# Dividing the softmax before its transposes, and a PSUM tile each for the gate and up products, in a two-layer diffusion trunk

## The chip, the cores and the metric

The kernel runs on one core of one Trainium2 chip. The metric is device time in microseconds (us), from the first to the last instruction of the program with what the runtime adds around it; a time given as "before" is the median of three runs. All data is float32 in the chip's main memory, about 480 MB of it read once.

## The reference, cut to what matters

Two layers run over 256 latent tokens and 256 context tokens of width 1024. Each layer projects the normalised tokens to three head groups (A: global attention of 6 heads, B: a 31-tap convolution with a normalisation behind it, C: windowed attention of 6 heads with a learned sink per head), multiplies their concatenation by `w_out`, adds it to the residual, and then applies a mixture of 32 experts, of which each token uses two. The last layer keeps only the latent tokens. What the change touches is the softmax and the first half of an expert:

```python
sc = jnp.einsum('bqhgd,bkhd->bhgqk', qblk, k_all).astype(jnp.float32) * ATTN_SCALE
p = jax.nn.softmax(sc, axis=-1).astype(v_all.dtype)
return jnp.einsum('bhgqk,bkhd->bqhgd', p, v_all)
...
def run(args):
    xb, e = args
    return (jax.nn.silu(xb @ w_gate[e]) * (xb @ w_up[e])) @ w_down[e]
```

## The kernel before, in words

**Layers and stages.** `layer(l)` is run for `l` = 0 and 1. In each: modulation and input projections; the attention stage; the output projection with `w_out` (line 952); the router; then 16 pairs of experts. Layer 0 handles four tiles of 128 tokens, layer 1 two.

**Attention.** `unit(g, j, i)` handles two heads (`h` = 0 and 1) of one block of queries. For `i` = 0 and 1 it is one latent block against 512 keys (`nb` = 1); for `i` = 2, in layer 0 alone, it is both context blocks against 256 keys each (`nb` = 2). Layer 0 has 18 units (12 with `nb` = 1, 6 with `nb` = 2), layer 1 has 12 (all `nb` = 1). TensorE makes the scores S (lines 819 to 822), VectorE takes their row maxima (825), ScalarE writes P = exp(S - max) and the row sums `lsum`, one head after the other (839), VectorE takes the reciprocals `rl` (848). TensorE transposes P by head (853), VectorE and ScalarE copy one head's PT each (854), TensorE multiplies by V into `po` (860). Two times `nb` more products by the identity spread `rl` along the free axis in the other half of `po` (866; each is two instructions). ScalarE copies that into `ars` (870), VectorE multiplies (871), and the result is split into a rounded high part (873, ScalarE) and a remainder (874, VectorE). The buffers of `ars` and `gpad`, the padded input of the convolution, lie in pools that close with the stage; line 1020 opens a pool for the weight tile `xs` after them, and its load (line 1021) is the first of a row of loads in SyncE's queue.

**What sets the order there.** SyncE's queue is in the order of the program. The other engines' order in the attention stage is chosen at build time by the framework's planner, from the order of the program and from its own estimate of when operands are ready. The convolution is 62 VectorE instructions on `gpad` and `ca` in a serial chain (`tap`, lines 641 and 643); those that are left when the units begin (`conv(len(taps))`, line 876) are spread among them. `conv_norm` follows with line 783 on the last tap, and its result is what the last two of eight parts of the output projection need.

**Expert pairs.** `pair` takes two experts, which use the two 64-column halves of the array. Weights come in tiles of 1 MB through a ring of eight, loaded ahead by SyncE; a slot is loaded again as soon as the products that read it are done. A pair uses 12 of them: four each for gate, up and down. The PSUM pool `P2` has two buffers of two banks each. Before the change one P2 tile `pgu` holds the gate product in its first bank and the up product in its second (line 1354), and another one, `py`, holds the down product (line 1408). ScalarE takes SiLU of the gate half (1358) when its 16 products are done; `burst(0)` then issues work of other pairs; the up products follow; VectorE multiplies both (1363); `split_y` (1275, 1276) empties `py`. In this loop the order on TensorE, VectorE and ScalarE is that of the program, and `burst(0)` to `burst(3)` mark the places where the gathers of the next quad and the scatter of the pair before are put. In layer 0, for pairs 1 to 13 of 0 to 15, `burst(0)` holds at most one VectorE instruction (`onehot`); in layer 1 it holds three scatter products of the pair before.

The framework adds the waits: an instruction that writes a tile waits for those that read or wrote that tile before, and a tile from a pool waits until the readers of the buffer's last tile are done.

Of the kernel before, what the change touches and what calls it, by code (L numbers as in the profile page):

```python
# [10 lines left out]
F32 = mybir.dt.float32  # L11
# [4 lines left out]
OP = mybir.AluOpType  # L16
# [20 lines left out]
def trunk(ctx: ExitStack, tc: tile.TileContext, t_in, rope, out, cfg):  # L37
# [426 lines left out]
    def layer(l):  # L464
# [343 lines left out]
        def unit(g, j, i):  # L808

            nb = 1 if i < 2 else 2
            S = P2("S")
            for b in range(nb):
                for h in range(2):
                    q, kv = qT[g](2 * j + h, 128 * (i + b)), (2 * j + h) // 3
                    masked = g == 1 and i < 2
                    o, ks = (S[:, h, :], slice(0, 512)) if i < 2 else (S[:, h, 256 * b:256 * b + 256], slice(256, 512))
                    pe.matmul(o, q, kH[g][:, kv, ks], start=True, stop=False)
                    pe.matmul(o, q, kL[g][:, kv, ks], start=False, stop=not masked)  # L820
                    if masked:
                        pe.matmul(S[:, h, 128 - 128 * i:256 - 128 * i], identb, masks[:, i], start=False, stop=True)
            n = 2 * nb
            mx = sm.tile([128, 4], F32, name="mx")[:, :n]
            ve.tensor_reduce(mx, S.rearrange("p h (b k) -> p (h b) k", b=nb), axis=AX.X, op=OP.max)
            nm = sm.tile([128, 4], F32, name="nm")[:, :n]
            ns = negsink[:, l, j, :, None].to_broadcast([128, 2, nb])
            if g == 1:
                ve.scalar_tensor_tensor(nm.rearrange("p (h b) -> p h b", b=nb), mx.rearrange("p (h b) -> p h b", b=nb),
                                        -SCALE, ns, op0=OP.mult, op1=OP.min)  # L830
            else:
                ve.tensor_scalar(nm, mx, -SCALE, None, op0=OP.mult)
            P = K4("P", (128, 2, 512))
            lsum = sm.tile([128, 4], F32, name="lsum")[:, :n]
            w_ = 512 // nb
            for h in range(2):
                for b in range(nb):
                    e = h * nb + b
                    sc.activation(P[:, h, w_ * b:w_ * b + w_], S[:, h, w_ * b:w_ * b + w_], AF.Exp,
                                  bias=nm[:, e:e + 1], scale=SCALE, accum_out=lsum[:, e:e + 1])  # L840
            if g == 1:
                es = sm.tile([128, 4], F32, name="es")[:, :n]
                ve.tensor_tensor(es.rearrange("p (h b) -> p h b", b=nb), nm.rearrange("p (h b) -> p h b", b=nb), ns,
                                 op=OP.subtract)
                sc.activation(es, es, AF.Exp)
                ve.tensor_tensor(lsum, lsum, es, op=OP.add)
            rl = sm.tile([128, 4], F32, name="rl")[:, :n]
            ve.reciprocal(rl, lsum)
            PT = K4("PT", (128, 2, 512))
            for h in range(2):  # L850
                pt = P1("pT")
                for kt in range(4):
                    pe.transpose(pt[:, 128 * kt:128 * kt + 128], P[:, h, 128 * kt:128 * kt + 128], ident)
                (sc.copy if h else ve.tensor_copy)(PT[:, h], pt)
            po = P1("po")
            for b in range(nb):
                for kt in range(4 // nb):
                    for h in range(2):
                        cv_ = 128 * g + 64 * ((2 * j + h) // 3)
                        pe.matmul(po[64 * h:64 * h + 64, 128 * b:128 * b + 128],  # L860
                                  V[:, kt if i < 2 else 2 + kt, cv_:cv_ + 64],
                                  PT[:, h, 128 * (b * 2 + kt):128 * (b * 2 + kt) + 128],
                                  start=kt == 0, stop=kt == 4 // nb - 1)
            for b in range(nb):
                for h in range(2):
                    pe.matmul(po[64 * h:64 * h + 64, 256 + 128 * b:384 + 128 * b],
                              rl[:, h * nb + b:h * nb + b + 1].to_broadcast([128, 64]), ident, start=True, stop=True)
            nq = 128 * nb
            rs = K2("ars", (128, nq), tag="a")
            sc.copy(rs, po[:, 256:256 + nq])  # L870
            ve.tensor_tensor(rs, po[:, 0:nq], rs, op=OP.mult)
            mh = qT[g](2 * j, 128 * i, nq)
            sc.copy(mh, rs)
            ve.tensor_tensor(qT[g](2 * j + 1, 128 * i, nq), rs, mh.bitcast(F32), op=OP.subtract)

        conv(len(taps))
        n = 0
# [466 lines left out]
        def pair(pr, xg, ws, burst, final, finish):  # L1344


            p = P2("pgu")
            for m in range(2):
                for a in range(2):
                    w_ = (load_rows_two([weights_of(pr, m, a, e) for e in range(2)], "we") if final else  # L1350
                          [weight(m, a, e, pr) for e in range(2)])
                    for k in range(4 * a, 4 * a + 4):
                        for e in range(2):
                            pe.matmul(p[64 * e:64 * e + 64, m, :], xg[:, k, 64 * e:64 * e + 64], w_[e](k % 4),  # L1354
                                      start=k == 0, stop=k == KC - 1)
                if m == 0:
                    sil = K2("sil", tag="w")
                    sc.activation(sil, p[:, 0], AF.Silu)  # L1358
                    if final:
                        sqrt_table(sil)  # L1360
                    burst(0)
            act = K2("act", tag="w")
            ve.scalar_tensor_tensor(act, p[:, 1], ws, sil, op0=OP.mult, op1=OP.mult)  # L1363
            burst(1)
            pt = P1("pat")
            for f in range(4):
                pe.transpose(pt[:, 128 * f:128 * f + 128], act.rearrange("s (a p k) -> s a k p", a=2, k=2)[:, f // 2, f % 2], ident)  # L1367
            actT = K2("actT", tag="w")
            sc.copy(actT, pt)  # L1369
            burst(2)  # L1370
            tiles = y_tiles()
            oht = K2("oht", (128, 512), F32R)

            def slots():
                pb = P1("pb")
                se = sm.tile([32, 2, 64], F32R, name="se")
                gp.tensor_copy(se, ident[:32, 2 * pr:2 * pr + 2, None].to_broadcast([32, 2, 64]))  # L1377
                pe.matmul(pb[:, :N], se.rearrange("p a b -> p (a b)"), posT[:, :N], start=True, stop=True)  # L1378
                ve.tensor_scalar(oht[:, :N], pb[:, :N], slotid, None, op0=OP.is_equal)

            def products(py, wd, fs):
                for f in fs:
                    for e in range(2):
                        pe.matmul(py[64 * e:64 * e + 64, :], actT[:, 128 * f + 64 * e:128 * f + 64 * e + 64],  # L1384
                                  wd[e](f), start=f == 0, stop=f == 3)

            slots()
            if final:
                for h in range(2):
                    py = P2("py")[:, 0]  # L1390
                    wd = load_rows_two([down_half(h, e, pr) for e in range(2)], "we")
                    products(py, wd, range(2))
                    if h == 0:
                        burst(3)
                    else:
                        finish(0, tiles, oht[:, :N], py)
                    products(py, wd, range(2, 4))
                    if h == 0 or not last:
                        split_y(py, h, 128, tiles)
                finish(1, tiles, oht[:, :N], py)  # L1400
                return []
            py = P2("py")
            for a in range(2):
                wd = [weight(2, a, e, pr) for e in range(2)]
                for f in range(2 * a, 2 * a + 2):
                    for h in range(2):
                        for e in range(2):
                            pe.matmul(py[64 * e:64 * e + 64, h], actT[:, 128 * f + 64 * e:128 * f + 64 * e + 64],  # L1408
                                      wd[e](f % 2)[:, 512 * h:512 * h + 512], start=f == 0, stop=f == 3)
                if a == 0:  # L1410
                    burst(3)
            for h in range(2):
                split_y(py[:, h], h, 128, tiles)
            return row_adders(tiles[0], tiles[1], oht[:, :N])
# [277 lines left out]
```

## Time and profile before

| what | value |
|---|---|
| median of 3 runs | 1475.16 us (1473.77 to 1477.0) |
| the profiled execution's own time | 1472.71 us |
| its span, first to last instruction | 1470.7 us |
| TensorE busy (matmul), share of the span | 1390.8 us, 95% |
| VectorE busy | 613.4 us, 42% |
| ScalarE busy | 395.7 us, 27% |
| mean granted TensorE clock | 0.986 |
| bytes read from main memory | 479.42 MB |

The profile is of one execution. A matmul's end is modelled and matmuls overlap, so TensorE's busy share says little about how full it is; the waits and the start times say more. PE stands for TensorE's matmuls, PEld for its weight loads, DVE for VectorE, ACT for ScalarE, POOL for GpSimd, SP for SyncE and its queue of loads. Layer 0's attention stage lies at about 142 to 240 us of the span, its expert pairs at about 300 to 800; layer 1's attention stage at about 895 to 950, its pairs at about 990 to the end.

### The profile page before, as it was taken

The numbers are of one execution on the slowest core, as the hardware profiler recorded it, in microseconds if no ns is written. First come the engines' busy times: TensorE is split into PE (matmuls) and PEld (weight loads), VectorE is DVE, ScalarE is ACT, GpSimd is POOL, SyncE is SP. The second block draws the span as 40 slices with busy tenths as digits, with TensorE's granted clock in tenths as the row PEclk, the third lists the DMA queues.
The fourth block names the chain that finished last, engine by engine and source line by source line (L and its number), as shares of the span: only waits on it lengthen the run. The fifth ranks groups of instructions, "written<-read, shape, count | busy, mean of one in ns | idle before, by whom it ended". The sixth has DMA issues, their size and how long they took to land. (4 is left out here: it accounts for less than half of the span.)

```text
span 1470.7 us, 20485 instructions
## 1 busy us (share of the span) xinstructions
PE 1390.8 (95%) x8068; PEld 771.3 (52%) x8068; DVE 613.4 (42%) x1380; ACT 395.7 (27%) x954; POOL 76.7 (5%) x132
## 2 busy tenths in 40 slices
PE   6999999999999999999998998889999999999987
PEld 5776677755445544444434776783433343333332
DVE  4379974443323423233325679853222222222223
ACT  4454675421111111101102565552111011111102
POOL 1202000100000000000001110010000000000000
PEclk9999999999999999999999999999999999999999
DMA  9757204397999999999999590186999999999996
GB/s 350 282 166 284 109 1 172 131 375 306 376 408 414 413 400 406 417 406 414 385 405 389 201 332 31 44 357 280 388 422 421 421 421 421 421 421 419 421 417 255
DMA packets 97412, 481.86 MB, mean 328 GB/s; under 512 B 14068, under 2 KB 22544, under 8 KB 52128
## 3 DMA queue, kind: packets, MB, share of 16 engines
q1 hardware_dynamic: 96576, 478.79, 81.1%
q8 instruction: 66, 1.08, 0.3%
q10 hardware_dynamic: 464, 1.11, 0.2%
q0 software_dynamic: 272, 0.59, 0.1%
q14 instruction: 34, 0.28, 0.0%
HBM read 479.42 MB, written 1.05 MB: 327 GB/s over the span
## 5 line engine op out<-in xcount | busy, mean ns | idle before, releaser
L1354 PE MATMUL pgu<-we,xg 128*64 128x512 f32 x1904 | 449.3, 598 | 30.7 <-DMA we<-in_w_gate_dram 13.6
L1354 PEld LDWEIGHTS pgu<-we,xg 128*64 128x64 f32 x1904 | 142.3, 137 | 324.1 <-issue 246.8
L1408 PE MATMUL py<-we,actT 128*64 128x512 f32 x888 | 202.9, 596 | 0.7 <-ACT actT L1369 0.7
L1363 DVE SCALAR_TENSOR_TENSOR act<-pgu,ws,sil 128x512 f32<-128x512 f32 x32 | 24.0, 751 | 285.1 <-PE pgu L1354 248.6
L1250 DVE SCALAR_TENSOR_TENSOR xT<-pc,mod,xT 128x256 f32<-128x256 f32 x256 | 104.8, 477 | 52.9 <-PE pc L1247 52.2
L1408 PEld LDWEIGHTS py<-we,actT 128*64 128x64 f32 x888 | 63.1, 137 | 117.5 <-issue 113.4
L1304 ACT COPY xg<-pg 128x256 f32<-128x256 f32 x112 | 36.3, 376 | 308.2 <-PE pg L1300 308.2
L1258 DVE TENSOR_TENSOR xo<-xo,pc 128x512 f32<-128x512 f32 x62 | 39.8, 684 | 112.0 <-PE pc L1257 112.0
L1299 PE MATMUL pg<-OH,hH 128*128 128x256 f32 x336 | 83.3, 286 | 0.0
L1300 PE MATMUL pg<-OH,hL 128*128 128x256 f32 x336 | 82.1, 283 | 0.0
L643 DVE SCALAR_TENSOR_TENSOR ca<-gpad,cw,ca 128x512 f32<-128x512 f32 (+1 forms) x120 | 74.2, 619 | 0.9
L1299 PEld LDWEIGHTS pg<-OH,hH 128*128 128x128 f32 x336 | 63.9, 190 | 7.2 <-issue 5.7
L1300 PEld LDWEIGHTS pg<-OH,hL 128*128 128x128 f32 x336 | 64.1, 191 | 0.9
L1358 ACT ACTIVATE sil<-pgu 128x512 f32<-128x512 f32 x32 | 19.1, 598 | 167.6 <-PE pgu L1354 167.6
L281 PE MATMUL pm<-wm,scT 128*32 128x256 f32 (+1 forms) x896 | 60.7, 359 | 3.0 <-DMA wm<-in_w_mod_dram 2.8
L1273 DVE TENSOR_TENSOR Yg<-py,g2r 128x512 f32<-128x512 f32 x31 | 21.3, 688 | 100.7 <-PE py L1408 96.4
L1276 DVE TENSOR_TENSOR YL<-py,YH 128x512 fp32r<-128x512 f32 x32 | 22.1, 690 | 92.7 <-ACT YH L1275 92.7
L1275 ACT CAST YH<-Yg 128x512 fp32r<-128x512 f32 x31 | 19.1, 617 | 141.2 <-DVE Yg L1273 141.2
L1275 ACT CAST YH<-py 128x512 fp32r<-128x512 f32 x32 | 18.7, 585 | 139.0 <-PE py L1408 113.8
L1377 POOL CAST se<-ident 32x128 fp32r<-32x128 f32 x32 | 9.1, 287 | 900.1 <-PE pb L1378 900.1
L1246 PE MATMUL pc<-oht,YH 128*128 128x512 f32 x128 | 53.4, 418 | 1.2 <-ACT YH L1275 1.2
L1247 PE MATMUL pc<-oht,YL 128*128 128x512 f32 x128 | 50.6, 395 | 0.2 <-DVE YL L1276 0.2
(429 smaller groups left out, 2106.0 us busy)
## 6 DMA issues: line engine op xcount, KB each, us to landing
we<-in_w_up_dram SPq DMA_DIRECT2D x112, 1024.0 KB, 9.7
we<-in_w_down_dram SPq DMA_DIRECT2D x111, 1024.0 KB, 12.4
we<-in_w_gate_dram SPq DMA_DIRECT2D x110, 1024.0 KB, 13.5
wm<-in_w_mod_dram SPq DMA_DIRECT2D x44, 1024.0 KB, 9.4
wp<-in_w_gate_dram SPq DMA_DIRECT2D x8, 1024.0 KB, 9.5
wp<-in_w_up_dram SPq DMA_DIRECT2D x8, 1024.0 KB, 9.7
we<-in_w_gate_dram SPq DMA_DIRECT2D x16, 512.0 KB, 12.1
we<-in_w_up_dram SPq DMA_DIRECT2D x16, 512.0 KB, 10.2
```

Source lines behind the costliest of these rows:

```text
L281: pe.matmul(p[0][32 * q:32 * q + 32], scT[:, kq, :], ws[128 * kq // nr][:, kq % (nr // 128), c:c + n], start=k == 0, stop=k == KC * nq // ...
L643: ve.scalar_tensor_tensor(a, g, wt, a, op0=OP.mult, op1=OP.add)
L1246: pe.matmul(pc, YH[:, 128 * o:128 * o + 128], oht, start=True, stop=False)
L1247: pe.matmul(pc, YL[:, 128 * o:128 * o + 128], oht, start=False, stop=True)
L1250: ve.scalar_tensor_tensor(xT[:, o, sl], pc[:, sl], mod[l][:, 5, o, s:s + 1], xT[:, o, sl], op0=OP.mult, op1=OP.add)
L1258: ve.tensor_tensor(xo[t][:, sl], xo[t][:, sl], pc, op=OP.add)
L1275: sc.copy(YH[:rows, sl], py)
L1299: pe.matmul(dst, hH[t][:, 128 * k:128 * k + 128], rhs, start=t == 0, stop=False)
L1300: pe.matmul(dst, hL[t][:, 128 * k:128 * k + 128], rhs, start=False, stop=t == NT - 1)
L1304: sc.copy(xg[e][:, k - 1:k + 1, :], v[:, :, e])
L1354: pe.matmul(p[64 * e:64 * e + 64, m, :], xg[:, k, 64 * e:64 * e + 64], w_[e](k % 4), start=k == 0, stop=k == KC - 1)
L1408: pe.matmul(py[64 * e:64 * e + 64, h], actT[:, 128 * f + 64 * e:128 * f + 64 * e + 64], wd[e](f % 2)[:, 512 * h:512 * h + 512], start=f == ...
```

## The change

In `unit`, P is multiplied by the reciprocals of its row sums in place, one head on VectorE and one on ScalarE, one instruction for each block, ahead of the transposes. The products that spread `rl`, the copy `ars` and the multiplication by it fall away; the high part is copied and the remainder is subtracted straight from `po` in PSUM. In `pair`, each of the gate and the up product gets a P2 tile of its own and uses its first bank.

```diff
             rl = sm.tile([128, 4], F32, name="rl")[:, :n]
             ve.reciprocal(rl, lsum)
+            for h in range(2):
+                for b in range(nb):
+                    e = h * nb + b
+                    p = P[:, h, w_ * b:w_ * b + w_]
+                    if h:
+                        sc.activation(p, p, AF.Identity, scale=rl[:, e:e + 1])
+                    else:
+                        ve.tensor_scalar(p, p, rl[:, e:e + 1], None, op0=OP.mult)
             PT = K4("PT", (128, 2, 512))
...
-            for b in range(nb):
-                for h in range(2):
-                    pe.matmul(po[64 * h:64 * h + 64, 256 + 128 * b:384 + 128 * b],
-                              rl[:, h * nb + b:h * nb + b + 1].to_broadcast([128, 64]), ident, start=True, stop=True)
             nq = 128 * nb
-            rs = K2("ars", (128, nq), tag="a")
-            sc.copy(rs, po[:, 256:256 + nq])
-            ve.tensor_tensor(rs, po[:, 0:nq], rs, op=OP.mult)
             mh = qT[g](2 * j, 128 * i, nq)
-            sc.copy(mh, rs)
-            ve.tensor_tensor(qT[g](2 * j + 1, 128 * i, nq), rs, mh.bitcast(F32), op=OP.subtract)
+            sc.copy(mh, po[:, 0:nq])
+            ve.tensor_tensor(qT[g](2 * j + 1, 128 * i, nq), po[:, 0:nq], mh.bitcast(F32), op=OP.subtract)
...
-            p = P2("pgu")
             for m in range(2):
+                p = P2("pgu")[:, 0]
                 for a in range(2):
...
-                            pe.matmul(p[64 * e:64 * e + 64, m, :], xg[:, k, 64 * e:64 * e + 64], w_[e](k % 4),
+                            pe.matmul(p[64 * e:64 * e + 64, :], xg[:, k, 64 * e:64 * e + 64], w_[e](k % 4),
                                       start=k == 0, stop=k == KC - 1)
                 if m == 0:
                     sil = K2("sil", tag="w")
-                    sc.activation(sil, p[:, 0], AF.Silu)
+                    sc.activation(sil, p, AF.Silu)
...
-            ve.scalar_tensor_tensor(act, p[:, 1], ws, sil, op0=OP.mult, op1=OP.mult)
+            ve.scalar_tensor_tensor(act, p, ws, sil, op0=OP.mult, op1=OP.mult)
```

## Rows read from the trace of the kernel before

**Rows 1.** The page's group of gate and up products: busy, mean ns, idle before.

```profile
L1354 PE MATMUL pgu<-we,xg 128*64 128x512 f32 x1904 | 449.3, 598 | 30.7 <-DMA we<-in_w_gate_dram 13.6 <-ACT sil L1358 10.3 <-DVEq L1454 3.8
```

**Rows 2.** Waits from 330 to 800 us (layer 0's pairs): total us, times, longest.

```profile
PE pgu L1354 <- ACT sil L1358: 10.3, 13, 1.1
...
PEld pgu L1354 <- DMA we<-in_w_up_dram: 1.1, 3, 0.6
```

**Rows 3.** Timeline, one pair of layer 0: start us, length us, idle before.

```profile
582.40 7.04 PE L1354 MATMUL pgu<-we,xg 128*64 128x512 f32 x32
...
584.60 0.69 DVE L1276 TENSOR_TENSOR YL<-py,YH 128x512 fp32r<-128x512 f32 x1 [0.65 <-ACT YH L1275]
...
589.57 0.60 ACT L1358 ACTIVATE sil<-pgu 128x512 f32<-128x512 f32 x1 [5.00 <-PE pgu L1354]
...
590.22 5.37 PE L1354 MATMUL pgu<-we,xg 128*64 128x512 f32 x24 [0.78 <-ACT sil L1358]
```

**Rows 4.** ScalarE's timeline, SiLU of four pairs, two of each layer.

```profile
404.38 0.60 ACT L1358 ACTIVATE sil<-pgu 128x512 f32<-128x512 f32 x1 [5.00 <-PE pgu L1354]
...
619.93 0.60 ACT L1358 ACTIVATE sil<-pgu 128x512 f32<-128x512 f32 x1 [5.00 <-PE pgu L1354]
...
1138.28 0.60 ACT L1358 ACTIVATE sil<-pgu 128x512 f32<-128x512 f32 x1 [5.84 <-PE pgu L1354]
...
1378.72 0.60 ACT L1358 ACTIVATE sil<-pgu 128x512 f32<-128x512 f32 x1 [5.96 <-PE pgu L1354]
```

**Rows 5.** Waits from 1030 us to the end (layer 1's pairs).

```profile
PEld pgu L1354 <- DMA we<-in_w_gate_dram: 32.3, 30, 2.2
```

**Rows 6.** Windows of pairs: PE, PEld, DVE, ACT, POOL busy, clock, DMA share, GB/s.

```profile
340.00:360.00 20.00, 20.00 (x127) 14.25 (x125) 8.30 (x21) 3.18 (x9) 0.29 (x1) 1.00 0.81 340
...
500.00:520.00 20.00, 20.00 (x111) 11.66 (x109) 8.35 (x21) 1.89 (x5) 0.29 (x1) 1.00 0.97 398
...
1140.00:1160.00 20.00, 19.39 (x91) 7.87 (x89) 3.30 (x6) 2.40 (x6) 0.29 (x1) 1.00 1.01 421
```

**Rows 7.** Single lines, both layers: ns min/median/max, first and last start.

```profile
L870 ACT COPY ars<-po x30: 266/266/373, 152.0 to 947.8; 128x128 f32<-128x128 f32 x24, 128x256 f32<-128x256 f32 x6
...
L871 DVE TENSOR_TENSOR ars<-po,ars x30: 265/292/425, 154.2 to 948.1; 128x128 f32<-128x128 f32 x24, 128x256 f32<-128x256 f32 x6
...
L641 DVE TENSOR_SCALAR ca<-gpad,cw,vb x4: 406/476/545, 89.2 to 907.4; 128x512 f32<-128x512 f32 x2, 128x256 f32<-128x256 f32 x2
...
L1592 ACT ACTIVATE fs<-xo,finr x2: 706/714/722, 1464.5 to 1465.1; 128x512 f32<-128x512 f32 x2
...
L839 ACT ACTIVATE P<-S,nm x72: 466/685/732, 145.5 to 934.7; 128x512 f32<-128x512 f32 x48, 128x256 f32<-128x256 f32 x24
```

**Rows 8.** PEld timeline, spreading of `rl` at the end of a unit of layer 1.

```profile
909.60 0.14 PEld L866 LDWEIGHTS po<-ident,rl 128*64 128x64 f32 x1
...
909.71 0.24 PEld L866 LDWEIGHTS po<-ident,rl 128*64 128x64 f32 x2
```

**Rows 9.** Windows of the attention stages, columns as in Rows 6.

```profile
188.00:218.00 30.00, 30.00 (x292) 23.24 (x293) 23.79 (x70) 21.75 (x74) 0.00 (x0) 1.00 0.01 2
895.00:905.00 10.00, 7.32 (x48) 6.14 (x48) 9.21 (x23) 5.61 (x17) 0.00 (x0) 0.67 0.01 2
...
895.00:948.00 53.00, 49.88 (x428) 39.15 (x429) 46.63 (x127) 32.03 (x94) 0.00 (x0) 0.94 0.01 2
```

**Rows 10.** DVE groups: taps from 188 to 224 us and from 895 to 948 us.

```profile
L643 DVE SCALAR_TENSOR_TENSOR ca<-gpad,cw,ca 128x512 f32<-128x512 f32 x1 | 0.7, 742 | 0.0
...
L643 DVE SCALAR_TENSOR_TENSOR ca<-gpad,cw,ca 128x256 f32<-128x256 f32 x42 | 20.1, 478 | 0.2
```

**Rows 11.** Timeline: layer 1's last taps, and PE behind `conv_norm`.

```profile
946.81 1.00 DVE L643 SCALAR_TENSOR_TENSOR ca<-gpad,cw,ca 128x256 f32<-128x256 f32 x2
...
954.98 0.43 PE L344 MATMUL cr<-ident,cn2r 128*128 128x128 f32 x2 [2.54 <-DVE cn2r L338]
```

**Rows 12.** SyncE's queue: what the load of `xs` waited for, both layers.

```profile
SPq L1021 <- DVE qT L874: 166.8, 2, 92.8
```

## Prediction

> **What bounds the kernel now.** I read the page first, then the waits of each stage, then start times, because a mean over the span mixes stages with different limits.
>
> The expert pairs are the larger part of the span. The page's group of gate and up products shows three things that their idle time waits for: weights, the SiLU, and a control instruction [rows 1]. The waits by stretch pull these apart. In layer 0 the products wait for the SiLU 13 times, and for weights 1.1 us in all [rows 2]; in layer 1 they wait for weights, 32.3 us for gate weights alone, and the SiLU is not in the list [rows 5]. So TensorE sets the pace in layer 0 and the loads set it in layer 1. The start times of the SiLU agree: seven pairs of layer 0 take 619.93 - 404.38 = 215.55 us, 30.79 each; eight pairs of layer 1 take 240.44 us, 30.06 each, at 421 GB/s [rows 4, 6].
>
> In the attention stages nothing is loaded: DMA share 0.01 [rows 9]. SyncE's next load waits for the end of the last unit [rows 12], and TensorE, VectorE and ScalarE pass work to each other. From 188 to 218 us TensorE is at 30.00 of 30 us, VectorE at 23.79, ScalarE at 21.75; VectorE is fullest in layer 1, 46.63 of 53 us, where it has 42 taps to run [rows 9, 10]. A microsecond lost or won here moves everything behind it.
>
> **The change part by part.**
>
> *The PSUM tiles.* In layer 0 the 32 gate instructions of a pair begin at 582.40 and end at 589.44, the SiLU runs from 589.57 to 590.17, and the first up product starts at 590.22 [rows 3]. The up weights are there (1.1 us of waiting in 13 pairs), and the up product writes the other bank; the wait is on the tile. With two tiles it goes. The gap shown is 0.78 us. Two column halves run side by side, so 16 pairs of instructions in 7.04 us are 0.44 us apart while one lasts 0.598 [rows 1, 3]: back to back, the next would start 0.16 us before the end of the last. The bubble is 0.78 + 0.16 = 0.94 us. It occurs in the 13 pairs 1 to 13 of layer 0 [rows 2]; in the others `burst(0)` puts TensorE work there.
>
> Upper bound of the gain: 13 x 0.94 = 12.2 us. Lower bound: if the loads hold each pair to layer 1's pace, 13 x (30.79 - 30.06) = 9.5 us. Early pairs have idle loads (share 0.81), later ones nearly none (0.97 at 398 GB/s, against 421) [rows 6], so the truth lies nearer the lower end: I take **-10.5 us**.
>
> What is late next: with two buffers and three tiles a pair, the up tile takes the buffer of the `py` before it and must wait for `split_y`. That ends at 584.60 + 0.69 = 585.29; the up products would start at 589.28, so 4.0 us of gate products cover it [rows 3]. The gate tile waits for the SiLU's product of the pair before, long done, as now.
>
> *Removed from a unit.* The spreading products: 2 x `nb` of two instructions each, on both column halves; loads of one half start 0.11 us apart [rows 8], so 0.22 us of TensorE for `nb` = 1 and 0.44 for 2. Layer 0: 12 x 0.22 + 6 x 0.44 = 5.3 us; layer 1: 12 x 0.22 = 2.6 us. ScalarE's copy: 0.266 or 0.373 us; VectorE's product: 0.292 or 0.425 [rows 7].
>
> *Added to a unit.* No multiplication of P is in the trace. VectorE's nearest row, a tensor by a per-partition scalar out of SBUF, takes 0.545 us for 512 elements and 0.406 for 256. ScalarE's nearest, an Identity with such a scale, takes 0.714 for 512; its exponentials give the shorter form, 0.466 at the least [rows 7]. VectorE, layer 0: 12 x 0.545 + 12 x 0.406 = 11.4, less 12 x 0.292 + 6 x 0.425 = 6.1, is +5.3 us; layer 1: 12 x (0.545 - 0.292) = +3.0. ScalarE, layer 0: 12 x 0.714 + 12 x 0.466 = 14.2, less 5.4, is +8.8; layer 1: +5.4. The high part and the remainder only change their source from SBUF to PSUM; lines 870 and 871 read `po` in PSUM at these widths at the price of lines 873 and 874, so nothing.
>
> The Trainium skill, "VectorE: DVE Perf Modes", section "Side-by-side", gives a float32 operation with one tensor source in SBUF two elements a cycle and some 150 cycles of start; that makes an estimated 0.43 us for 512 elements, and by it the 24 long ones would cost VectorE some 3 us less, and the sum below would be -10 to -12 us. The rows agree with the rate (0.139 us for the second 256 elements) and not with the start, so I keep them.
>
> *What of it is on the path.* Layer 0, from 188 us: TensorE sets the pace there, and the eight units that start in this stretch (three with `nb` = 2) take 5 x 0.22 + 3 x 0.44 = 2.4 us from it; VectorE's surplus for the same units is 5 x 0.253 + 3 x 0.387 = 2.4, ScalarE's 5 x 0.448 + 3 x 0.559 = 3.9, so 26.2 and 25.7 against TensorE's 27.6 of 30 us: still room [rows 9]. Before 188 us the taps fill VectorE (one tap is left after it [rows 10]), and the ten units there cost up to 5.3 - 2.4 = 2.9 us, unless taps move behind 188. Together about 0 for layer 0, bounds -5.3 and +5.3. Layer 1: if VectorE sets the pace, +3.0; if TensorE, -2.6. The last tap ends at 947.8 and `conv_norm` keeps TensorE waiting 2.54 us behind it [rows 11], so VectorE is the nearer one: +1.5. Attention together **+1.5 us**, bounds -7.9 and +8.3.
>
> *The memory behind `ars`.* Without `ars`, the tile `xs` can only lie over `gpad`, and its load waits for the last tap rather than the last line 874 [rows 12]. In layer 0 that is some 50 us earlier, but products there wait for no weights [rows 2]; in layer 1 taps and units end within 3 us of each other [rows 11]. Nothing, in both.
>
> Sum: -10.5 + 1.5 = **-9.0 us** on the profiled execution's own 1472.71 us, 1463.7. That execution lies 2.45 us under the median shown, so in terms of the median 1475.16 - 9.0 = **1466 us**.
>
> **The rivals.**
>
> *A. The longer chain stands open (slower).* Now head 0 is transposed while head 1's exponential runs. After the change both wait for that exponential (0.685), the reciprocal and the multiplication (0.545 or 0.714), and 0.266 + 0.292 us fall away at the end: about 0.8 us longer for a unit [rows 7]. For it: the planner fixes TensorE's order by its own estimates, and an in-order engine stands still at a transpose put too early. Against it: two score tiles let a second unit run meanwhile, and VectorE and ScalarE have room after 188 us. All 30 units open: 30 x 0.8 = +24, less 10.5, 1488 us. It decides from 13 units on (13 x 0.8 = 10.5). A milder form, some 8 open units in place of my +1.5, gives 1471.
>
> In the same place the clock may fall. From 895 to 905 us TensorE was busy 7.32 of 10 us, and its granted clock averaged 0.67, a mixture of its two levels, 2.4 and 1.2 GHz; over 188 to 218, with no idle piece, it was 1.00 [rows 9]. Worth about 3 us for each such stretch, it would come with A. The Trainium skill, "TensorE: Matmul & The Clock Gate", section "HAM oscillation", warns of gaps for this reason; the trace agrees in that stretch.
>
> *B. The pairs gain nothing.* Either the loads are already the limit in layer 0 (against it: 1.1 us of waiting, and 398 against 421 GB/s), or the wait for `split_y` takes the SiLU's place (against it: 4.0 us of cover), or the wait is on something that both tiles share, so that the change doesn't do what it says (against it: the SiLU is named 13 times). Then +1.5 us remains: 1477.
>
> *C. Attention gains too.* The planner uses TensorE's 5.3 + 2.6 us: -10.5 - 6 gives about 1458.5.
>
> **How the numbers follow.** Forecast 0.60, giving 1460 to 1471 with the attention stages within 4 us of the estimate; A mild 0.14 (1470 to 1474), A full 0.08 (1474 to 1490), B 0.09 (1473 to 1480), C 0.09 (under 1460). A measurement of this kernel tells 0.2%, 3 us, from no change: faster is under 1472.2, slower over 1478.1. Faster: 0.60 + 0.09 + 0.10 of A mild = 0.79. Same: 0.04 of A mild, 0.03 of A full, 0.05 of B = 0.12. Slower: 0.05 of A full and 0.04 of B = 0.09. The range leaves out A full, most of B and the far end of C: 1458 to 1474.5.
>
> **What would show it.** Right: no wait of line 1354 for 1358 in layer 0, an up product some 0.2 us before the SiLU starts, SiLU starts 29.9 to 30.1 us apart, layer 0's pairs shorter by about 10 us, waits for weights beginning to appear; attention stages within 4 us of their length, with VectorE and ScalarE fuller. Wrong: line 1354 waiting for 1276 or for weights by as much as it gains; transposes (853) waiting long for ScalarE or VectorE, with a lower clock beside them; or a pace of 30.8 as before.

## The result, and the profile after

The changed kernel took 1483.36 us in the median of five runs (1482.23 to 1487.56), the kernel before beside it 1475.16 us: a ratio of 1.0062, with a 95% interval of 1.0042 to 1.0083. It is 0.6% slower where 0.6% faster was forecast. The profiled execution of the changed kernel is its slowest one, 1487.56 us with a span of 1485.8 us, 15.1 us longer than the span profiled before. In its lines 1355 (before: 1354) are the gate and up products, 1359 SiLU, 854 and 856 the new multiplications on ScalarE and VectorE, 861 the transposes, 862 the copies of PT, 868 the products into `po`, 874 the rounded part.

**Where the time went.** The first and last SiLU of each layer cut the span into pieces. First the kernel before, then the changed one; of each the groups of SiLU (16 in each layer) and of the row maxima, the first step of VectorE in each unit (18 and 12), with ns min/median/max and first and last start:

```profile
L1358 ACT ACTIVATE sil<-pgu x16: 597/597/598, 313.7 to 772.1; 128x512 f32<-128x512 f32 x16
L1358 ACT ACTIVATE sil<-pgu x16: 597/598/602, 1001.9 to 1438.3; 128x512 f32<-128x512 f32 x16
L825 DVE TENSOR_REDUCE mx<-S x18: 1217/1225/1225, 143.5 to 215.4; 128x2 f32<-128x1024 f32 x12, 128x4 f32<-128x1024 f32 x6
L825 DVE TENSOR_REDUCE mx<-S x12: 1214/1218/1225, 874.1 to 931.7; 128x2 f32<-128x1024 f32 x12
```

```profile
L1359 ACT ACTIVATE sil<-pgu x16: 597/597/598, 329.6 to 777.0; 128x512 f32<-128x512 f32 x16
L1359 ACT ACTIVATE sil<-pgu x16: 597/598/600, 1017.1 to 1453.3; 128x512 f32<-128x512 f32 x16
L825 DVE TENSOR_REDUCE mx<-S x18: 1208/1224/1226, 144.4 to 226.9; 128x2 f32<-128x1024 f32 x12, 128x4 f32<-128x1024 f32 x6
L825 DVE TENSOR_REDUCE mx<-S x12: 1214/1222/1226, 879.7 to 946.6; 128x2 f32<-128x1024 f32 x12
```

Layer 0's pairs went from 458.4 to 447.4 us, 11.0 less. Layer 1's did not move (436.4, 436.2). The first SiLU of layer 0 comes 15.9 us later, and from the last SiLU of layer 0 to the first of layer 1 it takes 10.3 us more. Most of both lies in the units: from the first to the last maximum 71.9 us became 82.5 in layer 0 (17 steps, 4.23 us each, then 4.85), and 57.6 became 66.9 in layer 1. In layer 0 the added 10.6 us have two halves: the first five steps, up to about 170 us, went from 25.6 to 30.8 us, and the last twelve from 46.3 to 51.7, 0.45 us a step. The other 4.4 of the 15.9 us lie behind the last maximum. Layer 1's share is less sure: a kernel with the same units and the old pairs (softmax only, below) adds 5.7 us there and not 10.3.

**The pairs** did what the prediction said. Three views of the changed kernel answer to [rows 1 to 4]: the waits of TensorE from 330 to 800 us, the timeline of one pair, and the starts of two SiLU seven pairs apart.

```profile
PE pgu L1355 <- DVEq L1455: 1.5, 1, 1.5
...
PEld pgu L1355 <- DMA we<-in_w_up_dram: 4.3, 9, 1.1
```

```profile
593.46 12.61 PE L1355 MATMUL pgu<-we,xg 128*64 128x512 f32 x58
...
599.34 0.60 ACT L1359 ACTIVATE sil<-pgu 128x512 f32<-128x512 f32 x1 [5.00 <-PE pgu L1355]
```

```profile
418.31 0.60 ACT L1359 ACTIVATE sil<-pgu 128x512 f32<-128x512 f32 x1 [5.00 <-PE pgu L1355]
...
628.71 0.60 ACT L1359 ACTIVATE sil<-pgu 128x512 f32<-128x512 f32 x1 [5.00 <-PE pgu L1355]
```

SiLU is no longer among what the products wait for, and they run through its start without a break. Seven pairs take 210.40 us, 30.06 each: the pace of layer 1, which the loads set. Waits for up weights begin to show, 4.3 us where there were 1.1.

**The units** did not. TensorE's waits from 130 to 320 us, and two windows (columns as in [rows 6]; the first window also as it was before the change, ahead of it):

```profile
PE po L868 <- DVE PT L862: 6.6, 14, 1.1
PE S L819 <- ACT P L839: 6.1, 7, 2.1
...
PE pT L861 <- DVE P L856: 0.7, 2, 0.4
```

```profile
150.00:170.00 20.00, 17.66 (x171) 12.12 (x166) 17.99 (x33) 11.33 (x38) 1.26 (x1) 0.91 0.35 139
...
150.00:170.00 20.00, 16.02 (x111) 11.34 (x113) 19.46 (x35) 12.07 (x35) 1.62 (x1) 0.68 0.42 171
...
188.00:218.00 30.00, 26.14 (x216) 18.60 (x212) 21.94 (x55) 21.32 (x65) 0.00 (x0) 1.00 0.27 103
```

From 188 to 218 us TensorE had no idle piece before [rows 9]; now it is busy 26.14 of 30 us, and VectorE and ScalarE are not fuller (21.94 and 21.32, against 23.79 and 21.75). No engine is full there (from 150 to 170 us VectorE is, at 19.46 of 20). TensorE waits, and hardly at the transposes: it waits at the instructions queued behind them.

The whole stretch from 143 us to the first SiLU of layer 0, before and after:

```profile
143.00:313.70 170.70, 164.33 (x1272) 124.27 (x1271) 108.47 (x254) 94.81 (x252) 12.12 (x14) 0.98 0.34 132
...
143.00:329.60 186.60, 167.74 (x1179) 124.39 (x1178) 116.45 (x261) 102.70 (x259) 12.90 (x14) 0.95 0.33 123
```

TensorE is idle 6.4 us of it before and 18.9 after, so 12.5 of the 15.9 us are idle time. The rest is busy time, 3.4 us more for fewer instructions, at a lower mean clock. As a matmul's end is modelled, this division is rough.

TensorE's timeline over one unit of the steady stretch, first before the change, then after it:

```profile
209.44 0.66 PE L853 MATMUL pT<-ident,P 128*128 128x128 f32 x4
210.03 0.43 PE L860 MATMUL po<-PT,V 128*64 128x128 f32 x2
210.39 0.66 PE L853 MATMUL pT<-ident,P 128*128 128x128 f32 x4
210.80 0.47 PE L819 MATMUL S<-kH,qT 128*128 128x512 f32 x1
...
212.02 0.60 PE L853 MATMUL pT<-ident,P 128*128 128x128 f32 x4
```

```profile
210.52 1.09 PE L861 MATMUL pT<-ident,P 128*128 128x128 f32 x8
212.18 0.43 PE L868 MATMUL po<-PT,V 128*64 128x128 f32 x2 [0.57 <-DVE PT L862]
212.54 0.39 PE L819 MATMUL S<-kH,qT 128*128 128x256 f32 x1
...
213.69 1.09 PE L868 MATMUL po<-PT,V 128*64 128x128 f32 x14
214.71 1.09 PE L861 MATMUL pT<-ident,P 128*128 128x128 f32 x8
```

Before, four transposes of one head, the first products of that unit, which need the other head's copy, made some 2 us earlier, then four transposes of the next unit, then scores. After the change both heads become ready together, the planner puts all eight transposes in a row, and directly behind them the first product that needs their copy. Nothing stands between to cover the copy, and TensorE stands still 0.35 to 0.57 us there in nearly every unit of the steady stretch. As far as the traces of layer 0's units record it, eight transposes are followed directly by a product into `po` once before the change, and 14 times after it.

### The profile page after: what moved, and what is told of

Its sections match the earlier page's. It is cut to its first block, busy times and chain, and to the rows that moved or that the text cites. A ratio compares the mean times of both kernels' runs of the same rounds, so it can differ in the third digit from the quotient of the medians.

```text
span 1485.8 us, 20178 instructions
## 1 busy us (share of the span) xinstructions
PE 1395.6 (94%) x7924; PEld 777.3 (52%) x7924; DVE 622.1 (42%) x1386; ACT 407.8 (27%) x960; POOL 77.2 (5%) x132
## 5 line engine op out<-in xcount | busy, mean ns | idle before, releaser
L1355 PEld LDWEIGHTS pgu<-we,xg 128*64 128x64 f32 x1904 | 148.3, 137 | 308.1 <-issue 239.9
L868 PE MATMUL po<-PT,V 128*64 128x128 f32 x480 | 45.3, 297 | 9.5 <-DVE PT L862 9.1
## 6 DMA issues: line engine op xcount, KB each, us to landing
we<-in_w_up_dram SPq DMA_DIRECT2D x16, 512.0 KB, 10.2
```

Of the source, the lines that this page charges most:

```text
L868: pe.matmul(po[64 * h:64 * h + 64, 128 * b:128 * b + 128], V[:, kt if i < 2 else 2 + kt, cv_:cv_ + 64], PT[:, h, 128 * (b * 2 + kt):128 * ...
L1355: pe.matmul(p[64 * e:64 * e + 64, :], xg[:, k, 64 * e:64 * e + 64], w_[e](k % 4), start=k == 0, stop=k == KC - 1)
```

## The experiments

Each time is a median beside runs of the kernel before on the same chip (1472.9 us for the first four, 1473.7 for the next four, 1474.5 for the last three). The pieces are read from one trace each, as above, in us: to the first SiLU of layer 0, layer 0's pairs, from there to layer 1's first SiLU, layer 1's pairs.

| kernel | time | ratio to before, 95% interval | to layer 0's pairs | pairs 0 | between | pairs 1 |
|---|---|---|---|---|---|---|
| before | 1475.2 | 1 | 313.7 | 458.4 | 229.8 | 436.4 |
| the change | 1483.4 | 1.0062 (1.0042 to 1.0083) | 329.6 | 447.4 | 240.1 | 436.2 |
| tiles only | 1462.6 | 0.9918 (0.9896 to 0.9941) | 315.0 | 449.9 | 227.2 | 436.2 |
| softmax only | 1490.9 | 1.0109 (1.0087 to 1.0131) | 329.6 | 457.8 | 235.5 | 436.1 |
| thin | 1489.9 | 1.0096 (1.0067 to 1.0125) | 326.9 | 457.7 | 238.2 | 436.4 |
| rounded part on VectorE | 1490.0 | 1.0110 (1.0089 to 1.0130) | 326.6 | 457.6 | 234.3 | 435.9 |
| beside | 1479.1 | 1.0042 (1.0025 to 1.0059) | 318.6 | 457.7 | 231.4 | 436.3 |
| fronts ahead | 1470.8 | 0.9977 (0.9948 to 1.0005) | 315.0 | 457.6 | 227.6 | 436.1 |
| by head | 1487.0 | 1.0089 (1.0073 to 1.0106) | 323.0 | 457.8 | 237.0 | 436.4 |
| norm earlier | 1513.9 | 1.0278 (1.0261 to 1.0295) | 338.2 | 457.9 | 245.8 | 436.1 |
| the change, fronts ahead | 1458.0 | 0.9897 (0.9879 to 0.9915) | 314.8 | 447.4 | 225.5 | 436.2 |
| tiles, fronts ahead | 1457.2 | 0.9887 (0.9872 to 0.9902) | 311.8 | 448.3 | 225.8 | 436.3 |
| tiles only, again | 1462.0 | 0.9920 (0.9906 to 0.9933) | 311.8 | 448.3 | 227.8 | 435.8 |

The kernel run twice shows how far one trace's first piece can be off by itself: 315.0 and 311.8.

**The two halves apart.** The first kernel takes only the hunk in `pair`, the second only the hunks in `unit`.

> Only the PSUM tiles are changed; the softmax is as before. If the pairs' gain in the changed kernel's trace is the edit's own (10.9 us between the first and the last SiLU of layer 0), 1464 to 1466 us against 1475, ratio 0.993. Rival: the pairs were shorter only because a later start found their weights already loaded; then this kernel gains under 4 us.

> Only the softmax is changed; the pairs are as before. If the two edits add up, 1493 to 1501 us (ratio 1.012 to 1.018), with units of layer 0's steady stretch 4.2 to 4.5 us apart against 3.64. If the loss came from the two edits together, under 1485.

The tiles gain 1472.86 - 1462.63 = 10.2 us, about as expected, so a later start is not what made the pairs shorter. The softmax loses 1490.85 - 1472.86 = 18.0, a little less than expected; the sum, +7.8, is the whole change's +8.2. The last eight steps of layer 0 are 4.35 us apart, against 3.64 before. From here on, up to the last three, the kernels have the old pairs, so that only the softmax is judged.

**Is it the multiplications' length, or the engines' time?**

```diff
-                    p = P[:, h, w_ * b:w_ * b + w_]
+                    p = P[:, h, w_ * b:w_ * b + w_].rearrange("p (k c) -> p k c", c=128)[:, :, 0:1]
```

> The changed softmax with the old pairs, but each multiplication covers one column of each 128 and leaves the other 127 undivided: the transposes still wait for both heads' sums, and the multiplications are short. Theory C (the chain's length counts): both multiplications fall from 0.48 and 0.72 us to about 0.2, so the loss against before falls to 8 to 14 us. Theory F (full engines): the loss goes altogether, to under 4 us. Theory L (a loop in the engines' orders: ScalarE's rounded copy out of po stands ahead of the next unit's exponentials, and the products into po stand behind the score products that wait for those exponentials): no multiplication lies in that loop, the units stay 4.1 to 4.4 us apart in layer 0 and the loss stays at 17 us or more.

The multiplications, first of the changed kernel, then of this one:

```profile
L856 DVE TENSOR_SCALAR P<-P,rl x36: 346/480/489, 148.8 to 955.4; 128x512 f32<-128x512 f32 x24, 128x256 f32<-128x256 f32 x12
...
L854 ACT ACTIVATE P<-P,rl x36: 492/722/752, 148.3 to 955.5; 128x512 f32<-128x512 f32 x24, 128x256 f32<-128x256 f32 x12
```

```profile
L856 DVE TENSOR_SCALAR P<-P,rl x36: 220/226/232, 148.9 to 961.1; 128x4 f32<-128x4 f32 x24, 128x2 f32<-128x2 f32 x12
...
L854 ACT ACTIVATE P<-P,rl x36: 282/302/339, 148.4 to 961.2; 128x4 f32<-128x4 f32 x24, 128x2 f32<-128x2 f32 x12
```

Some 0.25 us less on one engine and 0.42 on the other in each long multiplication brought at most little: 17.0 us lost instead of 18.0. Theory F falls. Theory C's 8 to 14 us lie under the median, but the interval reaches down to 9.9 us lost, so a few us by the length of the multiplications are not excluded. The waits for the other head's exponential and for the reciprocal are still in this chain.

The counterpart keeps the work and takes the dependence away:

```diff
+            X = K4("X", (128, 2, 512))
+            for h in range(2):
+                for b in range(nb):
...
+                    if h:
+                        sc.activation(x, p, AF.Identity, scale=rl[:, e:e + 1])
+                    else:
+                        ve.tensor_scalar(x, p, rl[:, e:e + 1], None, op0=OP.mult)
             PT = K4("PT", (128, 2, 512))
```

> The kernel before with the same multiplications added, at the same place in the program, into a tile that nothing reads: VectorE and ScalarE have all the added work, and still the copy and the product that the change removes, but no transpose waits for it. Theory F (engine time) expects the loss of the softmax edit or more: 1490 us and above. Theory N (the transposes of both heads now come ready together; TensorE's order puts all eight of a unit in a row, and the first product into po directly behind them, with nothing to cover the copy of PT) expects at most a third of that loss: 1472 to 1479 us, with units 3.6 to 3.8 us apart.

It took 1479.06 us, 5.4 over before. In its window TensorE stays busy, though VectorE and ScalarE have more to do than in any other kernel here:

```profile
188.00:218.00 30.00, 29.03 (x281) 22.06 (x282) 26.88 (x73) 27.10 (x87) 0.00 (x0) 1.00 0.00 1
```

The last eight steps of layer 0 are 3.80 us apart. Both figures lie at the upper end of what theory N expected. So all the added engine time, with none of the removed work gone, costs 5.4 us; the larger part of the 18 comes with the dependence and the order that the planner makes of it.

**Which place in the order?** After the first traces a loop through ScalarE looked likely: the rounded part waits for `po` and stands ahead of the next exponentials, and `po` stands behind the scores that wait for those exponentials.

```diff
-            sc.copy(mh, po[:, 0:nq])
+            ve.tensor_copy(mh, po[:, 0:nq])
```

> The changed softmax with the old pairs, but VectorE makes the rounded copy out of po. Theory L: the copy no longer stands ahead of the exponentials, the loop is open, units 3.6 to 3.9 us apart, and the loss against before falls to 3 to 12 us. Theories C and F: nothing gets shorter and VectorE has 0.27 us more to do in each unit, so the loss stays at 18 to 28 us.

The loss stayed: 17.1 us. The loop was opened (the exponentials of a unit no longer follow a copy out of `po`), and TensorE still stands in the same place:

```profile
208.27 1.09 PE L861 MATMUL pT<-ident,P 128*128 128x128 f32 x8
209.93 0.43 PE L868 MATMUL po<-PT,V 128*64 128x128 f32 x2 [0.56 <-DVE PT L862]
210.29 0.39 PE L819 MATMUL S<-kH,qT 128*128 128x256 f32 x1
```

Theory L as stated falls as well; a loop through VectorE, which now makes this copy and also the row maxima, was not tested apart. Of the theories named, N is left: eight transposes in a row and an uncovered product behind them. It was tested by changing nothing but the order in which the program names the steps. `rest` is `unit` from the line of PT on.

```diff
-                    unit(g, j, i)
+                    held.append((g, j, i, *unit(g, j, i)))
+                    if len(held) > 1:
+                        rest(*held.pop(0))
...
+        rest(*held.pop(0))
         conv_norm()
```

> The changed softmax with the old pairs; same operations, but in program order a unit's scores, exponentials and multiplications stand ahead of the transposes and products of the unit before it, so that the planner finds other engine orders. If the loss is the length of a unit's own chain, nothing changes: 1488 to 1493 us. Theory N: it moves with the order; where the eight transposes and the first product into po have other work between them, the waits of po for PT fall from 9 us to under half in layer 0 and the time to 1476 to 1485 us.

It took 1470.79 us, 20 us less than the same operations in the other order, more than expected, and not to be told apart from the kernel before. TensorE's timeline, its waits from 188 to 230 us (first of softmax only, then of this kernel) and the maxima of layer 0:

```profile
206.88 1.09 PE L864 MATMUL pT<-ident,P 128*128 128x128 f32 x8
207.73 0.48 PE L819 MATMUL S<-kH,qT 128*128 128x512 f32 x1
...
209.04 0.66 PE L871 MATMUL po<-PT,V 128*64 128x128 f32 x8
```

```profile
PE po L868 <- DVE PT L862: 4.5, 10, 0.6
...
PE po L871 <- DVE PT L865: 1.4, 3, 0.7
```

```profile
L825 DVE TENSOR_REDUCE mx<-S x18: 1197/1220/1225, 144.6 to 212.2; 128x2 f32<-128x1024 f32 x12, 128x4 f32<-128x1024 f32 x6
```

The eight transposes are still in a row, but the scores of another unit (1.3 us) now stand between them and the products that need the copy. The units are 3.98 us apart instead of 4.85.

That cover is not the whole of the 20 us. From 143 us to the first SiLU, softmax only and this kernel:

```profile
143.00:329.60 186.60, 167.78 (x1178) 124.42 (x1178) 116.49 (x261) 102.75 (x258) 12.84 (x14) 0.95 0.33 123
...
143.00:315.00 172.00, 158.93 (x1181) 119.75 (x1172) 111.70 (x261) 102.31 (x259) 13.14 (x14) 0.97 0.35 133
```

Of the 14.6 us won back there, 5.7 are idle time of TensorE (the waits of `po` for PT fall from 6.6 to 2.8 us, those of the scores for P from 6.1 to 5.2), and 8.9 are shorter busy time for the same instructions. The mean clock rose with it; matmuls that follow each other closely also overlap more (eight transposes in a row take 1.09 us, where each lasts at least 0.27). No run separates these two. So the order is shown to be worth the 20 us, and the uncovered copy is one part of that.

The loads that now run during the units (DMA share 0.27 from 188 to 218 us, 0.01 before) do not explain the loss: this kernel has a share of 0.46 in that window.

Giving each head its own sum, reciprocal and multiplication was to pull the transposes apart instead:

```diff
-            ve.reciprocal(rl, lsum)
-            for h in range(2):
...
+            for h in range(2):
+                lsum = sm.tile([128, 2], F32, name=f"lsum{h}")[:, :nb]
...
+                rl = sm.tile([128, 2], F32, name=f"rl{h}")[:, :nb]
+                ve.reciprocal(rl, lsum)
```

> The changed softmax with the old pairs, but each head has its own sum, reciprocal and multiplication, so that head 0 is divided and can be transposed while head 1's exponential runs; VectorE and ScalarE have some more small instructions. Theory N: about half of the units get their transposes apart again (four and four), and half of the loss against before goes: 1479 to 1486 us. Theory F: more engine time, 1491 or more.

1487.0 us, 13.3 us lost where 18.0 were, less of a gain than expected; as the intervals overlap, it is not shown that any came back. In the planner's order some units have four and four transposes and others still eight. The last eight steps of layer 0 are 3.81 us apart again, near the 3.64 of before, so the pitch of the steady stretch is not the whole loss either.

A guess about the end of the stage went wrong:

```diff
+                    if n == (9 if last else 15):
+                        conv_norm()
...
-        conv_norm()
```

> The changed softmax with the old pairs, and the convolution's norm stands three units earlier in the program. In the trace with the change the last unit ends 9 to 10 us late, and the first SiLU of layer 0 another 5.6 us later, with TensorE waiting 2.5 us for the norm. If the norm's place behind the last unit costs that, 3 to 7 us come back: 1484 to 1488 us. If it does not, 1489 to 1493 us.

1513.9 us, 23 us worse than softmax only. ScalarE's timeline and TensorE's show where a good part of layer 0's share lies:

```profile
228.13 1.28 ACT L332 ACT_TABLE_LOAD   x1
...
230.46 1.28 ACT L798 ACT_TABLE_LOAD   x1
...
235.34 1.28 ACT L214 ACT_TABLE_LOAD   x1
...
236.84 1.28 ACT L839 ACT_TABLE_LOAD   x1
238.13 0.69 ACT L839 ACTIVATE P<-S,nm 128x512 f32<-128x512 f32 x1
```

```profile
239.63 0.58 PE L819 MATMUL S<-kH,qT 128*128 128x256 f32 x1 [7.62 <-ACT P L839]
```

The norm's functions take ScalarE in one piece, with four table loads of 1.28 us, ahead of the exponentials of the last units. This says nothing on where the norm's place in the changed kernel costs time; that guess was not tested by it.

**Is the division ahead of the transposes worth anything in a better order?** The next two have the new tiles and the fronts ahead, one with the new softmax and one with the old; the third is the first experiment again.

> The whole change, in the program order of the run with the fronts ahead. If the tiles' gain (10.2 us) and the reordered softmax (2.9 us under before) add up, 1459 to 1462 us, ratio 0.991. If the pairs' later or earlier start eats one of them, 1464 or more.

> The old softmax (division behind the products) with the new PSUM tiles, in that same program order. TensorE has the spreading products in it again, 5.3 us in layer 0 and 2.6 in layer 1. If the division ahead of the transposes is worth its TensorE time once the order suits it, this one is 3 to 8 us above the run of the whole change in that order: 1463 to 1468 us. If the program order alone is worth something for either softmax, it is within 2 us of it or below: 1457 to 1461 us.

> The PSUM tiles alone once more, old softmax in the old program order, beside the two others on one chip: 1461 to 1465 us. If the whole change with fronts ahead is the better kernel, it lies at least 1 us under this one.

The whole change in this order takes 1458.0 us, 1.03% under before. The old softmax in the same order takes 1457.2: the two cannot be told apart. So the division costs some 18 us in the old order and gains nothing in the new one, though it frees TensorE of the spreading products; the program order is worth 4.8 us to the old softmax too (0.9887 with an interval up to 0.9902, against 0.9920 from 0.9906), so most of the 20 us belong to the new softmax in the old order. The best kernel found is the old softmax with the new tiles and the fronts ahead.

## Why the prediction was wrong

**The PSUM tiles: right, in place and size.** -10.5 us was forecast from 13 bubbles of 0.94 us and the loads' pace; the half alone measured -10.2, and -12.5 when it was run again. The signs named for the pairs came: no wait for SiLU, no break at its start, a pace of 30.06, the first waits for up weights. The wait for `split_y` does not show. Rival B is refuted.

**The softmax: the step that failed is "what of it is on the path".** It summed engine time, found room on VectorE and ScalarE and TensorE relieved, and took +1.5 us with bounds of -7.9 and +8.3. Measured: +18.0, outside the bounds. In the steady stretch the room was there and is there still (21.94 and 21.32 of 30 us); it was the wrong thing to count, since 5.4 us is all that more work on those engines cost (beside). The step took the order of TensorE's queue as given. In the steady stretch TensorE had no idle piece before the change, so the order there covered every copy with something else. The edit made both heads ready at one moment, and the planner wrote a new order without that cover: up to layer 0's pairs TensorE is idle 12.5 us more, 6.6 of them at products that wait for PT. The same operations in another order took 20 us less.

**Rival A named the right stage and nearly the size, with a wrong place.** It priced the longer chain at 0.8 us for each unit, +24, and 1488 us with the tiles; it had a chance of 0.08. But it put the stall at the transposes, which wait 0.7 us in all layer 0, and priced it by the length of the chain, of which the multiplications, cut short, gave back 1.0 us at the median (thin). That its 1488 us came near is luck in part. Its reason against, "VectorE and ScalarE have room", was no reason: here TensorE waited with room on both.

**The clock** fell in that stage, as A's second part feared: from 150 to 170 us the granted clock averaged 0.68 of full speed, a mixture of 2.4 and 1.2 GHz, where it was 0.91 before, with TensorE busy 16.02 of 20 us. An estimate from the two windows above: 0.95 over 186.6 us lacks 9.3 us of full speed and 0.98 over 170.7 lacks 3.4, so the clock is at most some 6 of the 15.9 us. From 188 to 218 us it was 1.00 before and after, so the half of the loss in the later steps is not the clock's. No run here holds the clock and lets the order change.

**Prices of single instructions** were near. VectorE's multiplication took 0.480 us for 512 elements where 0.545 was used, ScalarE's 0.722 where 0.714 was. The Trainium skill, "VectorE: DVE Perf Modes", section "Side-by-side", gave an estimated 0.43 for VectorE's, so the measured 0.480 lies between it and the row I took. The thin kernel, whose multiplications are shorter by more than that difference, is not clearly faster.

**The memory behind `ars`** did what was said: the load of `xs` in layer 0 starts at 180.67 us, as the last tap ends, instead of some 60 us later, and the piece before the pairs is no shorter for it.

```profile
179.91 0.73 DVE L643 SCALAR_TENSOR_TENSOR ca<-gpad,cw,ca 128x512 f32<-128x512 f32 x1
...
180.67 0.34 SPq L1022 DMA_DIRECT2D xs<-in_w_down_dram  x1
```

**What stays open:** the split of the loss between the copy of PT and the scores that wait for P (6.6 and 6.1 us in layer 0), the clock and the shorter busy time; the 4.4 us behind layer 0's last maximum, where TensorE waits 2.5 us for the convolution's norm; layer 1's share; and why the new program order gains the old softmax 4.8 us, whose steady stretch had no idle TensorE to win back.

## What to carry to other kernels

When an edit changes what an instruction waits for, look at what is queued directly behind it on its engine, and ask what covers the time from its end to the copy that the next one needs; free time on other engines was no answer here. Where a planner writes the order, a new dependence can rewrite the order of the whole stage: try the same operations under another program order before the edit is judged, and the old ones too. A bubble between two halves of one PSUM tile can be priced from one timeline (the gap, plus the piece by which neighbouring products otherwise overlap) and held against the next limit, here the loads.

## What was not expected of the hardware

VectorE and ScalarE at 26.88 and 27.10 busy of 30 us, each in a chain with TensorE, still let TensorE be busy 29.03 of 30 (beside). And 20 us, over 1% of the kernel, lay in the program order of the same instructions, with 8.9 us of TensorE's busy time among them.
